# A two-layer block with a recurrent and a dilated-attention mixer: the first half of attention's output projection enters the planned order, and the conditioning loads are woven in further apart

## The chip, the cores and the metric

The kernel runs on one core of a Trainium2 chip. The metric is the device time of one execution in microseconds (us). Three runs of the kernel before gave 1509.72, 1512.40 and 1514.42 us; the median is 1512.4 us.

## What is computed

512 tokens of 1024 features pass through two layers. Layer 0 mixes with a gated linear recurrence (HGRN), layer 1 with an attention in which each of 8 heads has three groups (a near window and two strided ones) whose outputs are merged by their softmax sums. Each layer ends in a SwiGLU feed-forward net with 2816 hidden features. A vector `c` conditions both layers: `ada_w` turns it into six vectors of 1024 a layer (a shift, a scale and a gate for the mixer, and the same three for the feed-forward net).

```
cond = silu(c)
for layer in (0, 1):
    sh1, sc1, g1, sh2, sc2, g2 = split(cond @ ada_w[layer] + ada_b[layer], 6)
    u = rms_norm(h, norm_g[layer, 0]) * (1.0 + sc1) + sh1
    y = hgrn2_mixer(u, ...) if layer == 0 else dilated_attention_mixer(u, ...)
    h = h + (1.0 + g1) * rms_norm(y, norm_g[layer, 1])
    u = rms_norm(h, norm_g[layer, 2]) * (1.0 + sc2) + sh2
    y = (silu(gate) * up) @ ffn_w_out[layer]      # gate, up = split(u @ ffn_w_in[layer])
    h = h + (1.0 + g2) * rms_norm(y, norm_g[layer, 3])

def dilated_attention_mixer(u, cos, sin, w_in, w_out):
    proj = (u @ w_in).reshape(B, S, N_GROUPS, 3, ATT_HEADS, ATT_HEAD_DIM)
    for gi, (window, dilation) in enumerate(DILATED_GROUPS):
        q, k, v = rope(proj[:, :, gi, 0]) * scale, rope(proj[:, :, gi, 1]), proj[:, :, gi, 2]
        o_g, lse_g = dilated_group_attention(q, k, v, window, dilation)
    wts = softmax(stack(lses), axis=0)
    o = einsum('gbsh,gbshd->bshd', wts, stack(outs))
    return o.reshape(B, S, D_MODEL) @ w_out
```

## The kernel before

**Number format.** Every large product runs on TensorE (PE) in three passes of single-precision parts: a matrix `x` is cut into a high part (a cast, on ScalarE, ACT) and a low part (the difference, on VectorE, DVE), and `three` issues high·high, high·low and low·high into one PSUM bank. So each weight needs a load, a cast and a subtraction before PE can use it, and each operand of the output projection needs one cast (`oh`, a head's high part) and one subtraction (`ol`, its low part, named `oT` in the trace because it takes the place of an `oT` tile).

**Weights.** `items` is one list for the whole kernel: the order in which loads of about 1 MB are issued on SyncE's queue (SP) into a ring of two places called `raw`. A load starts only when the last reader of the item two places ahead in the list is done. Kinds of items are `w` (1 MB at once), `quarters`, `half`, `rows` and `ada`. An `ada` item is conditioning work: 1 MB of `ada_w`, four multiply-and-adds of 128x512 on DVE (lines 390 and 392; lines 1965 and 1967 within the plan). Behind every second `ada` comes a sum over the partitions on GpSimd (POOL), `partition_all_reduce` (line 394, or 1970 in the plan), and then four small turns into a column on DVE (line 404) or, for a gate, a `rows` load and two adds. `weave(ws, others, first, every)` strews the groups of `others` among the weights `ws`: one behind each `every`-th weight.

**Stages**, in the profile's time: the recurrence of layer 0 with its output turn (to about 300 us), its feed-forward net (to about 700 us), attention's products (q, k and v for 3 groups and 8 heads) and heads from about 740 to 1103 us, attention's output turn (1103 to about 1170 us), and the second feed-forward net.

**The recurrence's output turn.** `mixer_out` multiplies the eight heads (kt = 0 to 7) by the output weights; the last two heads still come through `core_c`/`core_d` while the first products run. `core_d` needs a mean square over a head raised to the power -1/2, which POOL does with `pow` (line 590, tile `orr`); a vector op on DVE (tile `aT`, line 1615) follows and PE turns the result (line 1622). A lone row `ISA` on POOL in the orders below is the instruction that changes POOL's loaded program between `partition_all_reduce` and `pow`.

**Attention's order.** An object `plan` is given every task of attention with its engine, an estimated cost and what it reads and writes, and derives one fixed order for each engine from it. Scores, merges, flips (turns on PE) and sums of a head are added at `ticks`, one for each q/k unit of groups 1 and 2. The plan ends with the last q/k products of head 7 and two of the four output weights. The rest, the "tail", is written by hand in `mixer_out` (its `else` branch and the dictionary `tail`): first half of the output turn, `y0` (four banks, one for each 128 tokens, first 512 columns), eight products kt for each; between them what is left of heads 6 and 7: the sums `pv_n(6)`, the scores `scores(7, 2)`, merges, flips and sums of head 7, and the way back of `h` from its place in memory (`back`). `y1` is the second half of the columns; its first bank is worked before kt = 7. The high parts `oh` stand in two places: three where the operand parts `up` were, and five that open when the q/k places (`mkx`) close behind kt = 0.

Of the kernel before, what the change touches and what calls it, by code (L numbers as in the profile page):

```python
# [10 lines left out]
F32 = mybir.dt.float32  # L11
F32R = mybir.dt.float32r
# [4 lines left out]
P = 128  # L17
# [274 lines left out]
def block_kernel(tc, x, c, positions, ada_w, ada_b, norm_g, hgrn_w_in, lower, hgrn_norm_g, hgrn_w_out,  # L292
# [8 lines left out]
    with ExitStack() as ctx:  # L301
# [250 lines left out]
        woven(late[:6], 2)  # L552
# [4 lines left out]
        woven(late[6:], 2)  # L557
        items += [wtok(attn_w_out[0], kq, hf * 512) for hf in range(2) for kq in range(2)]
# [126 lines left out]
        def mixer_out(oT, otp, groups, gate, l, side, close, tail=None):  # L685


            aux = ExitStack()
            oh, ol = [], []

            def parts(n):
                uid[0] += 1
                pp = aux.enter_context(tc.tile_pool(name=f"parts{uid[0]}", bufs=1, side=bass.opposite_side(side)))
                place = not oh
                for _ in range(n):
                    oh.append(fresh(pp, [P, S], f"oh{len(oh)}", 1, F32R))
                if place:
                    pp.tile([P, 72], F32, name=f"pad{uid[0]}")

            def cut(kt):  # L700
                ol.append(fresh(otp, [P, S], *(("oT", 7) if kt < 7 else ("oT_late", 2)), F32R))
                split(oh[kt], ol[kt], oT[kt])

            parts(groups[0])
            y0 = [bank("mm") for _ in range(NT)]
            y1 = {}
# [12 lines left out]
            if tail is None:  # L719
                for kt in range(KT):  # L720
                    if kt % 4 == 0:
                        w = st.take()
                    cut(kt)
# [3 lines left out]
            else:  # L727
                with tc.manual_schedule(engines=ORDERED):
                    for kt in range(3):
                        cut(kt)  # L730
                    for kt in range(KT):
                        if kt % 4 == 0:
                            w = st.take(0)
                        if kt == KT - 1:
                            ws = [st.take(0), st.take(0)]
                            mm(0, range(7))
                        for t in range(NT):
                            prods(y0[t], t, kt, w)
                        if kt == 0:
                            for fn in tail[-1]:  # L740
                                fn()
                            parts(groups[1])
                        if kt < 4:
                            cut(kt + 3)
                        for fn in tail.get(kt, ()):
                            fn()
                        if kt == 6:
                            cut(7)
                        if kt in (4, 5):
                            for hi_f, lo_f in st.pieces(2, True):  # L750
                                hi_f()
                                lo_f()
                            st.fill()
# [7 lines left out]
            mm(0, range(8) if tail is None else (7,))  # L761
# [912 lines left out]
        first = mixer_out(oT, otp, (8,), gates.pop((0, 2)), 0, "left", lambda: None)  # L1674
# [277 lines left out]
        acc_of = {}  # L1952
# [49 lines left out]
        def products(cost, dst, key, terms, begin, reads):  # L2002


            def go():
                todo = [p for t in terms() for p in t]
                for i, (x, y) in enumerate(todo):
                    pe.matmul(dst(), x, y, start=begin and i == 0, stop=i == len(todo) - 1, skip_group_check=True)  # L2008
            PE(cost, go, reads, [key])
# [399 lines left out]
        steps, after = [], []  # L2409
# [19 lines left out]
        for _ in range(2):  # L2429
            raw, p = next_weights(), plan.place("hl", 3, lambda: st.part_tiles(0))  # L2430
            for n in range(2):
                two = slice(n * 1024, n * 1024 + 1024)
                ACT(1.0, lambda raw=raw, p=p, two=two: act.copy(p.t[0][:, two], raw.t[:, two]), [raw()], [p("h", n)], goal=clock[0])
                DVE(1.15, lambda raw=raw, p=p, two=two: dve.tensor_sub(p.t[1][:, two], raw.t[:, two], p.t[0][:, two].bitcast(F32)),
                    [raw(), p("h", n)], [p("l", n)], goal=clock[0])
            done_with_raw()
            after.append(p)
        with tc.manual_schedule(engines=ORDERED | {mybir.EngineType.SP}):
            planned = plan.run()
        st.ready += [tuple(p.t) for p in after]  # L2440
        st.done, st.taken = at_item[0], st.taken + sum(k == "qk" and not by_seven(g) for k, g, _ in order)
        for st_ in heads.values():
            for name, p in st_.items():
                if isinstance(p, Place):
                    st_[name] = p.t
        for name, p in gates.items():
            if isinstance(p, Place):
                gates[name] = p.t
        upx.close()
# [36 lines left out]
```

## Time and profile before

| | before |
|---|---|
| median of 3 runs (lowest, highest) | 1512.4 us (1509.72, 1514.42) |
| the profiled execution: its time, its span | 1514.89 us, 1513.2 us |
| mean granted TensorE clock | 0.992 |
| PE busy | 1485.4 us, 98% |
| DVE, ACT, POOL busy | 1111.0, 795.5, 198.8 us |
| 20 us stretches in which PE is least busy | 280 to 300 us, 1100 to 1120 us, 800 to 820 us |

The span runs from the first to the last instruction; the execution's time has 1.7 us around it. PE is busy in 98% of the span, so the time can be read as PE's work plus the places where PE stands still, plus those where its granted clock is low; the list of PE's waits names each place with the engine and the line that ended it.

### The profile page before, as it was taken

Reading aid. Unit: us, or ns where it says so; the run is one execution under the profiler, and the core shown is the slowest. Engines: PE = TensorE matmul, PEld = TensorE weight load, DVE = VectorE, ACT = ScalarE, POOL = GpSimd, SP = SyncE. Lnnn points to the kernel's source line nnn. Section 1 sums busy time; section 2 is a strip of 40 time slices with the busy share of each in tenths; the row PEclk is TensorE's granted clock in tenths of the full one; section 3 lists DMA queues with packets and bytes.
Section 4 is the critical chain, followed back from the end, with each engine's and each line's share of the span. In section 5 each row is a group of like instructions: output and inputs, shape, how many; then the busy total and the mean of one; then the engine's idle time right before and its main releaser. Section 6 shows DMA issues by size and latency. Waiting matters only on the chain. (4 is left out here: it accounts for less than half of the span.)

```text
span 1513.2 us, 25135 instructions
## 1 busy us (share of the span) xinstructions
PE 1485.4 (98%) x9807; PEld 1329.2 (88%) x9807; DVE 1111.0 (73%) x1906; ACT 795.5 (53%) x1472; POOL 198.8 (13%) x174
## 2 busy tenths in 40 slices
PE   8999999899999999999999999999999999999998
PEld 6777888788999987888998999999978899999886
DVE  4587868387788876768798888888766978887533
ACT  4433443273555542366647777568865555555231
POOL 1011211130111101130001101001002211110100
PEclk9999999999999999999999999999999999999999
DMA  9554445215333347624244434443323333334531
GB/s 308 183 166 140 153 139 187 92 60 165 96 112 112 112 140 238 227 84 167 88 143 139 113 118 133 120 134 95 92 99 125 94 102 113 112 110 142 195 112 56
DMA packets 210152, 201.09 MB, mean 133 GB/s; under 512 B 8249, under 2 KB 167921, under 8 KB 209777
## 3 DMA queue, kind: packets, MB, share of 16 engines
q1 hardware_dynamic: 207056, 192.71, 40.9%
q10 hardware_dynamic: 1952, 6.65, 1.2%
q8 instruction: 77, 1.26, 0.4%
q0 software_dynamic: 1024, 0.13, 0.2%
q14 instruction: 43, 0.34, 0.1%
HBM read 192.31 MB, written 5.31 MB: 131 GB/s over the span
## 5 line engine op out<-in xcount | busy, mean ns | idle before, releaser
L89 ACT CAST hi<-raw 128x2048 fp32r<-128x2048 f32 x43 | 82.1, 1909 | 151.4 <-DMA raw<-in_ffn_w_out_dram 72.5
L90 DVE TENSOR_TENSOR lo<-raw,hi 128x2048 fp32r<-128x2048 f32 x43 | 101.8, 2371 | 62.5 <-ACT hi L89 62.3
L575 PE MATMUL ps_mm<-uh,hi 128*128 128x512 f32 (+1 forms) x400 | 146.4, 366 | 0.0
L576 PE MATMUL ps_mm<-ul,hi 128*128 128x512 f32 (+1 forms) x400 | 144.4, 361 | 1.0 <-DVE ul L675 1.0
L577 PE MATMUL ps_mm<-uh,lo 128*128 128x512 f32 (+1 forms) x400 | 144.7, 362 | 0.0
L2008 PE MATMUL ps_mm<-apart,hiq 128*128 128x256 f32 (+1 forms) x608 | 142.6, 327 | 0.0
L2008 PEld LDWEIGHTS ps_mm<-apart,hiq 128*128 128x128 f32 x608 | 99.9, 189 | 8.1
L2008 PE MATMUL ps_mm<-apart,loq 128*128 128x256 f32 (+1 forms) x304 | 98.0, 322 | 0.1
L990 PE MATMUL ps_mm<-th,loq 128*128 128x256 f32 x340 | 94.0, 277 | 0.0
L990 PE MATMUL ps_mm<-tl,hiq 128*128 128x256 f32 x340 | 94.0, 277 | 0.0
L990 PE MATMUL ps_mm<-th,hiq 128*128 128x256 f32 x340 | 94.0, 277 | 0.0
L981 DVE TENSOR_TENSOR loq<-raw,hiq 128x1024 fp32r<-128x1024 f32 x68 | 80.3, 1223 | 18.6 <-ACT hiq L977 18.6
L575 PEld LDWEIGHTS ps_mm<-uh,hi 128*128 128x128 f32 x400 | 75.6, 189 | 19.8 <-issue 8.4
L576 PEld LDWEIGHTS ps_mm<-ul,hi 128*128 128x128 f32 x400 | 75.6, 189 | 12.0 <-DVE ul L675 1.4
L577 PEld LDWEIGHTS ps_mm<-uh,lo 128*128 128x128 f32 x400 | 75.5, 189 | 11.4
L961 POOL TENSOR_TENSOR raw<-raw 128x512 f32<-128x512 f32 x34 | 44.9, 1320 | 305.3 <-DVE spare L957 149.6
L575 PE MATMUL ps_mm<-hi,oh 128*128 128x512 f32 x208 | 82.0, 394 | 1.0 <-ACT hi L89 1.0
L576 PE MATMUL ps_mm<-lo,oh 128*128 128x512 f32 x208 | 82.1, 395 | 0.2 <-DVE lo L90 0.2
L2008 PE MATMUL ps_mm<-uh,hiq 128*128 128x256 f32 x256 | 73.4, 287 | 3.7 <-ACT ps_mm L2100 2.5
L977 ACT CAST hiq<-raw 128x1024 fp32r<-128x1024 f32 x68 | 68.1, 1049 | 15.7 <-DVE raw L965 14.8
L2008 PE MATMUL ps_mm<-uh,loq 128*128 128x256 f32 x256 | 72.4, 283 | 0.2 <-DVE loq L2054 0.2
L2008 PE MATMUL ps_mm<-ul,hiq 128*128 128x256 f32 x256 | 72.4, 283 | 0.0
(513 smaller groups left out, 4668.1 us busy)
## 6 DMA issues: line engine op xcount, KB each, us to landing
raw<-in_ada_w_dram SPq DMA_DIRECT2D x40, 1024.0 KB, 5.2
raw<-in_ffn_w_in_dram SPq DMA_DIRECT2D x136, 256.0 KB, 3.6
raw<-in_ffn_w_out_dram SPq DMA_DIRECT2D x22, 1024.0 KB, 5.0
raw<-in_attn_w_in_dram SPq DMA_DIRECT2D x64, 256.0 KB, 4.8
raw<-in_hgrn_w_in_dram SPq DMA_DIRECT2D x12, 1024.0 KB, 5.3
raw<-in_attn_w_in_dram SPq DMA_DIRECT2D x12, 1024.0 KB, 5.2
raw<-in_ffn_w_in_dram SPq DMA_DIRECT2D x10, 1024.0 KB, 5.1
raw<-in_attn_w_in_dram SPq DMA_DIRECT2D x16, 512.0 KB, 5.3
```

The source lines that it names most:

```text
L89: self.nc.scalar.copy(hi, t)
L90: self.nc.vector.tensor_sub(lo, t, hi.bitcast(F32))
L575: pe.matmul(ps, ah, bh, start=start, stop=False, skip_group_check=part)
L576: pe.matmul(ps, ah, bl, start=False, stop=False, skip_group_check=part)
L577: pe.matmul(ps, al, bh, start=False, stop=stop, skip_group_check=part)
L961: pool.tensor_add(r[:, 2], r[:, 2], r[:, 0])
L977: act.copy(hi, src)
L981: dve.tensor_sub(lo, src, hi.bitcast(F32))
L990: pe.matmul(ps, w[x][:, a], us[kt][y], start=begin and kt + m == 0, stop=kt == 3 and m == 2, skip_group_check=True)
L2008: pe.matmul(dst(), x, y, start=begin and i == 0, stop=i == len(todo) - 1, skip_group_check=True)
```

## The change

Three lists are woven otherwise, and the tail becomes tasks of the plan.

1. In the recurrence's output turn the four loads of layer 1's FFN scale, `(1, 4)`, are called `shift`. The first of them now precedes the output weights, and the others follow one to each weight (before: two to a weight from the second on). The last column work goes into the plain weights of the feed-forward net, and that net's gate loads come one item later.
2. In attention four groups instead of six are woven into heads 1 to 4, one for each 2.5 items instead of 2; two into heads 5 to 7, one for each 3; the last two `ada` loads are woven into the four output weights.
3. The first half of attention's output turn is added to the plan: casts of the four output weights, the parts `oh`/`ol`, the products of `y0` and seven of `y1[0]`, the ways back of `h`. All eight high parts are in one place, that of `up` (`apart`), opened when all products of q, k and v (`of_units`) are done. What the plan holds of heads 6 and 7 comes at ticks inside this loop. `merged`, `flipped` and `sums` are the functions that the other heads already use, so head 7's merges run as scalings on ACT (before in the tail: on DVE), and its flips are copied on ACT.

```
-        items += weave(hg, ada_seq((0, 2), (0, 4), (0, 3)), 1)
-        items += weave(hg_o, [g for g in ada_seq((1, 4)) if g], 0, 0.5)
+        shift = ada_seq((1, 4))
+        items += weave(hg, ada_seq((0, 2), (0, 4), (0, 3)), 1) + shift[0]
+        items += weave(hg_o, shift[1:4], 0)
...
-        items += weave(f0a[:n0], gate_loads[:2] + [gate_fins[:1]], 2) + f0a[n0:]
+        items += weave(f0a[:n0], shift[5:] + gate_loads[:2] + [gate_fins[:1]], 2) + f0a[n0:]
...
-        woven(late[:6], 2)
+        woven(late[:4], 2.5)
...
-        woven(late[6:], 2)
-        items += [wtok(attn_w_out[0], kq, hf * 512) for hf in range(2) for kq in range(2)]
+        woven(late[4:6], 3)
+        out_w = [wtok(attn_w_out[0], kq, hf * 512) for hf in range(2) for kq in range(2)]
+        items += weave(out_w, late[6:], 0)
...
+        def out_weights():
             raw, p = next_weights(), plan.place("hl", 3, lambda: st.part_tiles(0))
             for n in range(2):
                 two = slice(n * 1024, n * 1024 + 1024)
+                ACT(1.0, lambda two=two: act.copy(p.t[0][:, two], raw.t[:, two]), [raw()], [p("h", n)])
+                DVE(1.15, lambda two=two: dve.tensor_sub(p.t[1][:, two], raw.t[:, two], p.t[0][:, two].bitcast(F32)), [raw(), p("h", n)], [p("l", n)])
             done_with_raw()
+            ws.append(p)
...
+        def out_cut(kt):
+            ACT(0.58, lambda: act.copy(oh[kt], oT[kt]), [("oT", kt), rows_of[kt]], [("oh", kt)])
...
+        out_weights()
+        out_weights()
+        open_parts(8, of_units, upx.close)
+        for kt in range(3):
+            out_cut(kt)
+        y0 = [mm_of() for _ in range(NT)]
+        last = ticks.n
+        for kt in range(KT):
+            if kt == 7:
+                y1[0] = mm_of("a")
+                for k in range(7):
+                    out_prods(y1[0], 0, k, ws[2 + k // 4])
+            for t in range(NT):
+                out_prods(y0[t], t, kt, ws[kt // 4])
+            for _ in range({0: 3, 2: 1, 4: 1, 5: 1, 6: 1}.get(kt, 0)):
+                ticks.tick()
+            if kt == 0:
+                come_back(0, [("PN", 0, t) for t in range(NT)])
+            if kt < 4:
+                out_cut(kt + 3)
...
+            if kt in (4, 5):
+                out_weights()
```

How the order moves, at three places. **POOL in the recurrence's output turn** (`shared` is the sum of one half of the conditioning vector, `orr` is the `pow` of heads 6 and 7). Before:

```order
L394 ISA
L394 ISA shared<-shared 128x512
L590 ISA
L590 TENSOR_TENSOR orr_2308<-rv_2309,expo 128x4
L394 ISA
L394 ISA shared<-shared 128x512
L590 ISA
L590 TENSOR_TENSOR orr_2342<-rv_2343,expo 128x4
```

With the change:

```order
L394 ISA
L394 ISA shared<-shared 128x512 x2
L592 ISA
L592 TENSOR_TENSOR orr_2315<-rv_2316,expo 128x4
L592 TENSOR_TENSOR orr_2349<-rv_2350,expo 128x4
```

Both sums now stand ahead of both `pow`, and one pair of program changes is gone; head 6's `pow` waits for the second sum.

**DVE at the start of attention's output turn** (`loq` is the low part of an output weight, `oT<-oT,oh` the low part of a head, `mR` the maxima of head 7's scores, `rot` and `shared` the rotary rows of head 7). Before:

```order
L2281 TENSOR_SCALAR nN_10183<-sN_10528 128x4
L2434 TENSOR_TENSOR loq_10843<-raw_10695,hiq_10842 128x1024
L2434 TENSOR_TENSOR loq_10931<-raw_10962,hiq_10930 128x1024
L572 TENSOR_TENSOR oT_11081<-oT_6093,oh_11071 128x512
L572 TENSOR_TENSOR oT_11084<-oT_6094,oh_11072 128x512
L572 TENSOR_TENSOR oT_11087<-oT_6095,oh_11073 128x512
L2434 TENSOR_TENSOR loq_10931<-raw_10962,hiq_10930 128x1024
```

With the change:

```order
L2256 TENSOR_SCALAR nN_10137<-sN_10530 128x4
L1939 TENSOR_SCALAR shared<-raw_10947,cond 128x512
L1941 SCALAR_TENSOR_TENSOR shared<-raw_10947,cond,shared 128x512 x2
L2426 TENSOR_TENSOR oT_11046<-oT_6093,oh_11018 128x512
L1941 SCALAR_TENSOR_TENSOR shared<-raw_10947,cond,shared 128x512
L1995 STREAM_SHUFFLE rot_10973<-shared 128x256
L1996 TENSOR_TENSOR rot_10973<-rot_10973,shared 128x256
L1997 TENSOR_TENSOR shared<-shared 128x256
L1998 TENSOR_TENSOR shared<-shared,rot_10973 128x256
L2412 TENSOR_TENSOR loq_10824<-raw_10682,hiq_10823 128x1024
L2426 TENSOR_TENSOR oT_11078<-oT_6094,oh_11019 128x512
```

Four steps of conditioning now stand around the first low part, and the second half of the first weight's low part and the rotation of head 7's rows stand ahead of the second. The second output weight (`raw_10962`, now `raw_11080`) comes some 25 instructions later.

**DVE in the middle of that turn**, where head 7's first merge (`wM`, `wE`, `wZ`) stands, with the change:

```order
L2412 TENSOR_TENSOR loq_10915<-raw_11080,hiq_10914 128x1024
L1941 SCALAR_TENSOR_TENSOR shared<-raw_11082,cond,shared 128x512
L2298 TENSOR_TENSOR wM_10835<-sR_10407,oR_10405 128x4
L2299 TENSOR_TENSOR wE_10895<-sR_10407,wM_10835 128x4
L2300 TENSOR_TENSOR wE_10895<-oR_10405,wM_10835 128x4
L1941 SCALAR_TENSOR_TENSOR shared<-raw_11082,cond,shared 128x512
L2412 TENSOR_TENSOR loq_10915<-raw_11080,hiq_10914 128x1024
```

Before, no conditioning stood here: the merge followed three low parts of heads.

```order
L572 TENSOR_TENSOR oT_11140<-oT_6096,oh_11135 128x512
L572 TENSOR_TENSOR oT_11155<-oT_6097,oh_11136 128x512
L572 TENSOR_TENSOR oT_11170<-oT_6098,oh_11137 128x512
L1834 TENSOR_TENSOR wM_11173<-sR_10429,oR_11120 128x4
L1835 TENSOR_TENSOR wE_11174<-sR_10429,wM_11173 128x4
L1836 TENSOR_TENSOR wE_11174<-oR_11120,wM_11173 128x4
```

The merge now stands behind the arrival of a second conditioning load (`raw_11082`), which the ring of two places lets start only behind an output weight.

More of the change, by code (lines that the diff above doesn't have):

```diff
@@ L760, in mixer_out @@
             n.gated(0, 0)
-            mm(0, range(8) if tail is None else (7,))
+            mm(0, range(8) if made is None else (7,))
             n.sq_y(0, 1)
@@ L2438, in block_kernel @@
+        while st.items[at_item[0]][0] in ("ada", "do", "rows"):
+            condition(st.items[at_item[0]])
+            at_item[0] += 1
         with tc.manual_schedule(engines=ORDERED | {mybir.EngineType.SP}):
             planned = plan.run()
[L2440 to L2445, printed above, removed]
```

113 lines of the change are left out of this document (51 added, 62 removed).

## The prediction

> **What bounds the kernel now.** First the page's table of busy time:
>
> ```profile
> PE 1485.4 (98%) x9807; PEld 1329.2 (88%) x9807; DVE 1111.0 (73%) x1906; ACT 795.5 (53%) x1472; POOL 198.8 (13%) x174
> ```
>
> PE stands still for 1513.2 - 1485.4 = 27.8 us of the span. The change removes no product, so it can only gain from those 27.8 us and from stretches at a low granted clock, and can only lose by making more of either. The list of PE's waits says where they are (engine, line, what ended the wait; us in all, times, longest):
>
> ```profile
> PE ps_a L1622 <- DVE aT L1615: 4.8, 1, 4.8
> PE ps_mm L2008 <- ACT ps_mm L2100: 2.5, 1, 2.5
> ...
> PE ps_mm L575 <- ACT qk L2112: 2.0, 1, 2.0
> ...
> PE ps_mm L2008 <- ACT ps_mm L2096: 1.1, 1, 1.1
> ...
> PE ps_mm L575 <- ACT oh L571: 0.9, 1, 0.9
> PE ps_mm L2008 <- DVE loq L2188: 0.8, 1, 0.8
> PE ps_a L2298 <- ACT h L2363: 0.7, 1, 0.7
> ```
>
> These seven lie in the three places that the change touches: the recurrence's output turn (4.8), attention's products (2.5, 1.1, 0.8) and the start of attention's output turn (2.0, 0.9, 0.7). I sum the change place by place. A difference of 0.3%, 4.5 us, is about what a measurement of this kernel can tell from no change.
>
> **Attention's output turn.** PE there, then the turn by stretches (length, busy time of PE, PEld, DVE, ACT, POOL, granted clock, DMA share, GB/s):
>
> ```profile
> 1103.09 0.93 PE L2355 MATMUL ps_a<-ident,h 128*128 128x128 f32 x7
> 1104.91 0.50 PE L575 MATMUL ps_mm<-hiq,oh 128*128 128x512 f32 x1 [0.89 <-ACT oh L571]
> 1106.32 1.91 PE L2298 MATMUL ps_a<-qk,qk 128*128 128x128 f32 x8 [0.68 <-ACT h L2363]
> 1111.92 0.50 PE L575 MATMUL ps_mm<-hiq,oh 128*128 128x512 f32 x1 [1.98 <-ACT qk L2112]
> ...
> 1146.91 0.39 PE L577 MATMUL ps_a<-hi,oT_late 128*128 128x512 f32 x1
> 1147.14 0.39 PE L575 MATMUL ps_a<-hi,oh 128*128 128x512 f32 x1
> ```
>
> ```profile
> 1106.00:1108.00 2.00, 1.68 (x9) 1.68 (x9) 1.79 (x4) 1.98 (x5) 0.00 (x0) 0.63 0.93 309
> 1108.00:1110.00 2.00, 1.94 (x6) 1.03 (x4) 1.97 (x8) 1.96 (x7) 0.00 (x0) 0.51 0.52 203
> ...
> 1112.00:1114.00 2.00, 2.00 (x9) 1.72 (x10) 0.00 (x0) 1.95 (x6) 0.00 (x0) 0.84 0.87 322
> 1114.00:1116.00 2.00, 2.00 (x12) 2.00 (x10) 0.00 (x0) 0.15 (x1) 0.00 (x0) 0.50 0.00 0
> 1116.00:1118.00 2.00, 2.00 (x14) 1.91 (x14) 1.00 (x4) 0.00 (x0) 0.55 (x1) 0.81 0.02 1
> ```
>
> From the last flips of the planned part (1103.09) to the first product of the second token group's second half (1147.14) pass 44.05 us. Three waits take 0.89 + 0.68 + 1.98 = 3.55 us. The low clock costs, in each stretch PE's busy time by what the clock lacks of 1, 0.62 + 0.95 + 0.32 + 1.00 + 0.38 = 3.27 us. Without both, the same instructions take 37.2 us, so -6.8 us is the most that this place can give.
>
> What the planned order puts in their place: the 1.98 us wait was for a bank that still held a q/k product, which ACT read behind four exponentials; with the change ACT's reads of those banks stand around the first `oh`, ahead of the exponentials, so this wait goes. The first products of kt = 0 now stand behind the scores and `pv_n(6)`, which gives `oh` and `ol` the time of those. The costs that come in are DVE's and POOL's:
>
> ```profile
> 1116.74 0.69 DVE L1901 TENSOR_TENSOR oT_late<-oT_late,ps_b 128x512 f32<-128x512 f32 x1 [5.16 <-PE ps_b L1900]
> ```
>
> ```profile
> 795.73 2.32 DVE L1967 SCALAR_TENSOR_TENSOR shared<-raw,cond,shared 128x512 f32<-128x512 f32 x3
> ```
>
> ```profile
> raw<-in_ada_w_dram SPq DMA_DIRECT2D x40, 1024.0 KB, 5.2
> ```
>
> Each of the two conditioning loads adds four steps of 0.77 us on DVE (the row above, 2.32 / 3), so 6.2 us, and some 2 us of column work. DVE has idle time for it here, 5.16 us in the first row alone. What counts is the queue. Walking each engine's new order with the durations of before: `pv_n(6)` waits about 0.5 us for the copy of its flips, since ACT casts the first `oh` ahead of it; the second `ol`, behind four steps of conditioning, the rotation of head 7's rows and the second half of the first weight, comes about 0.4 us after PE asks. Head 7's first merge stands behind the second conditioning load. That load waits on SP behind an output weight, which waits for the place of the first (free at about 1110); two loads of 1 MB from there, 5.2 us the first and about 3.3 us more the second, land it at about 1118.5; the merge and its scalings end at about 1124.6, just when PE comes to head 7's flips. The last two weights then land some 4 us ahead of their products. The sum over the partitions that follows at about 1124.4 meets the low part of head 6, the third cost. What it does to DVE shows earlier (POOL's sum, then DVE's rows beside and behind it):
>
> ```profile
> 867.57 3.23 POOL L1970 PARTITION_ALL_REDUCE shared<-shared  x1 [12.75 <-DVE shared L1967]
> ```
>
> ```profile
> 867.86 2.22 DVE L2021 TENSOR_TENSOR rot<-rot,shared 128x256 f32<-128x256 f32 x1
> 870.01 0.41 DVE L2022 TENSOR_TENSOR shared<-shared 128x256 f32<-128x256 f32 x1
> ```
>
> An instruction of 0.41 us takes 2.22 us beside the sum, and ends 0.7 us before it. So head 6's low part is late by about 2 us, and PE, which has 1 us of other work there, waits about 1.1 us. Together 0.5 + 0.4 + 1.1 = 2.0 us: the place costs -6.8 + 2.0 = **-4.8 us**. Its bounds are -6.8 (nothing waits) and +2.9, from the row below: DVE's 23.9 us of work between 1103 and 1141 become 23.9 + 8.2 + 2.1 (beside the sum) - 2.2 (head 7's scalings, now on ACT) = 32.0 us. Its idle time is 38 - 23.9 = 14.1 us now; if only the 5.16 us of it go, the 38 us become 32.0 + 8.9 = 40.9.
>
> ```profile
> 1103.00:1141.00 38.00, 34.45 (x178) 29.22 (x177) 23.85 (x66) 22.23 (x49) 2.63 (x4) 0.91 0.38 128
> ```
>
> [...]
>
> **The recurrence's output turn.** POOL and PE before:
>
> ```profile
> 268.26 1.68 POOL L590 TENSOR_TENSOR orr<-rv,expo 128x4 f32<-128x4 f32 x1 [9.17 <-DVE rv L589]
> 275.87 3.25 POOL L394 PARTITION_ALL_REDUCE shared<-shared  x1 [5.94 <-PE ps_b L1608]
> 286.30 1.05 POOL L590 TENSOR_TENSOR orr<-rv,expo 128x4 f32<-128x4 f32 x1 [7.18 <-issue]
> ```
>
> ```profile
> 273.44 0.61 PE L1606 MATMUL ps_b<-v_tok,aT 128*128 128x128 f32 x4
> ...
> 288.13 1.12 PE L1622 MATMUL ps_a<-ident,aT 128*128 128x128 f32 x4 [4.79 <-DVE aT L1615]
> ```
>
> Between the end of the sum (279.12) and the `pow` lie 7.18 us in which POOL waits for nothing else: the price of the program change. Before, head 6 had its `pow` ahead of the second sum and only head 7 paid. Now the order is sum, sum, change, `pow`, `pow`, and head 6 pays. The second sum needs the fourth conditioning load. By the same kind of walk its place in the ring comes free at about 258.8; with 5.2 us of landing and DVE's queue behind it, a weight's low part of 2.3 us among it, its last step ends at about 271.3. The sum then takes 3.25, the change 7.18, the `pow` 1.05 to 1.68, DVE's product 0.69 (as the 128x512 one in the row at 1116.74): 283.5 to 284.1. PE comes to the turn at about 277.4 (273.44, 1.5 us of `core_c`, eleven products at 0.23 us, as 1146.91 to 1147.14), and waits 6.1 to 6.7 us; I take 6.7 instead of 4.79, since the `pow` right behind a change was the longer one. Head 7 then finds its value ready, and the clock behind the wait I take as before. Cost **+2 us**; bounds -1 (the load lands early and DVE's queue is clear) and +4 (landing 2 us later).
>
> **Attention's products.** The 2.52 us wait:
>
> ```profile
> 805.59 0.39 PE L2008 MATMUL ps_mm<-uh,hiq 128*128 128x256 f32 x1 [2.52 <-ACT ps_mm L2100]
> ```
>
> ```profile
> 800.67 1.84 DVE L2021 TENSOR_TENSOR rot<-rot,shared 128x256 f32<-128x256 f32 x1
> ```
>
> ```profile
> 807.00:809.00 2.00, 2.00 (x12) 2.00 (x11) 1.93 (x4) 1.53 (x6) 0.00 (x0) 0.50 0.54 142
> ```
>
> ACT's copy of a bank stood behind copies of rotary rows that DVE finished late: its first step took 1.84 us instead of 0.4 beside POOL's sum. The wait and the low clock in the last row (2.00 us at 0.50) cost 3.5 us; with the waits of 1.1 and 0.8 the block can give 5.4. With six loads instead of eight, DVE has 6.2 us less here, the sums fall elsewhere, and the weights behind the second load start one item earlier. But sums and loads remain, and one may hit another narrow place. I take the 3.5 as gained and 1.0 as returned (the size of the second wait): **-2.5 us**; bounds -5.4 and +2.5 (one more wait like the first).
>
> [...]
>
> Where the gate loads of the first feed-forward net come one item later, PE works with no wait in the list, and the weights come at about the same time: 0.
>
> **Sum.** -4.8 + 2 - 2.5 = -5.3 us: the profiled execution's 1514.89 us would be 1509.6, and the median 1512.4 us **1507**.
>
> **The rivals.**
> - *The small terms all fall well*: the recurrence's wait does not grow (0), the tail loses 0.5, the block's waits go (-5): 1501. For it: each cost worked out above is a wait of about 1 us, within the error of the walk. Against it: three would have to vanish.
> - *The tail is given back in part*: the second conditioning load lands 2 to 3 us later, as it would behind two full landings of 5.2 us (1120.4), and head 7's flips wait with it; -2.5 there, +2 and -0.5 elsewhere: 1511.4. For it: the merge has no slack. Against it: two loads in flight landed faster than one by one.
> - *DVE becomes the bound of the tail*, and the kernel is slower. Its place: the queue that now mixes eight steps of conditioning, four weights' halves, eight low parts and head 7's merges. Its price: the +2.9 above, with the clock halved once behind its waits (1.7, as from 1112 to 1118), +2 in the recurrence and 0 in the block: 1512.4 + 2.9 + 1.7 + 2 = 1519. It decides if DVE keeps about 9 of its 14.1 us of idle time, because each instruction waits for a load or for PE in an order made from estimates. For it: the estimates know neither the clock nor the 2 us beside a sum. Against it: most of the new work is there early and could fill that idle time.
>
> **How the numbers follow.** Forecast 0.40, all well 0.20, given back in part 0.18, DVE-bound 0.22. Faster by over 4.5 us means under 1507.9: 0.28 of the forecast's 0.40, all 0.20 and 0.02 make 0.50. Slower means over 1516.9: 0.20 of the DVE case and 0.05 of given back make 0.25; the rest is 0.25. The range of 8 in 10 goes from 1500 to 1518; the forecast's own is 1503 to 1511.
>
> **What would show it.** Right: in the list of PE's waits the one for ACT `qk` is gone, the turn lasts about 39 us between the same two products, the clock there stays at 1; on POOL two sums follow each other and PE's wait for `aT` is about 7 us; around 805 us PE does not stand. Wrong: PE waits of over 1 us for `loq` or `oT` low parts or for head 7's flips in the turn, with DVE waiting for `raw`; or a wait of over 2 us at a new place between 780 and 1000 us.

## The result, and the profile after

The changed kernel takes 1511.49 us (median of 12 runs, 1508.44 to 1513.67) against 1513.76 us for the kernel before (12 runs, 1509.72 to 1516.32): a ratio of 0.9987 with a 95% interval of 0.9976 to 0.9998. That is 2.3 us less. The interval lies just below 1, and the gain is smaller than the 0.3% (4.5 us) which the prediction took as the least that can be told from no change. The forecast was 5.3 us less.

The profiled execution took 1511.48 us, its span 1509.5 us at a mean granted clock of 0.995 (before 1514.89, 1513.2 and 0.992). The page's table of busy time after the change:

```profile
PE 1481.1 (98%) x9807; PEld 1324.4 (88%) x9807; DVE 1108.2 (73%) x1896; ACT 799.6 (53%) x1482; POOL 200.7 (13%) x174
```

PE now stands still for 1509.5 - 1481.1 = 28.4 us, and before for 27.8: the change took no idle time away from PE on balance. Its busy time fell by 4.3 us for the same 9807 products, because less of it ran at a low clock (mean granted clock 0.995 instead of 0.992). The list of PE's waits (engine, line, what ended the wait; us in all, times, longest; line numbers here are some 26 lower than before):

```profile
PE ps_a L1596 <- DVE aT L1589: 5.1, 1, 5.1
PE ps_mm L1982 <- ACT ps_mm L2071: 2.9, 2, 2.1
...
PE ps_a L2330 <- DVE sN L2253: 1.8, 1, 1.8
...
PE ps_a L2330 <- ACT h L2319: 0.9, 1, 0.9
```

Of the seven waits quoted before, two at the start of attention's output turn are gone: the 2.0 us for ACT's `qk` and the 0.9 us for `oh`. The third one there, 0.7 us for `h`, is down to 0.2. The wait for `aT` in the recurrence is 5.1 us instead of 4.8. Attention's products have a wait of 2.1 us of the same kind as the one of 2.5 before, and a new one of 1.8 us.

To see where the time went I cut the span at five of PE's products, the same ones in each kernel. In the kernel before (PE's timeline; start, duration, then the idle time ahead of it and what ended it):

```profile
25.57 0.74 PE L1345 MATMUL ps_a<-hi,uh 128*128 128x512 f32 x2 [0.61 <-ACT uh L1320]
330.54 1.10 PE L656 MATMUL ps_b<-ident,xn 128*128 128x128 f32 x8 [0.56 <-DVE xn L650]
599.19 0.50 PE L575 MATMUL ps_mm<-hi,oh 128*128 128x512 f32 x1 [0.99 <-ACT hi L89]
```

and with the change:

```profile
27.49 0.74 PE L1319 MATMUL ps_a<-hi,uh 128*128 128x512 f32 x2 [0.61 <-ACT uh L1294]
331.69 1.09 PE L658 MATMUL ps_b<-ident,xn 128*128 128x128 f32 x8 [0.56 <-DVE xn L652]
600.55 0.50 PE L577 MATMUL ps_mm<-hi,oh 128*128 128x512 f32 x1 [0.72 <-ACT hi L89]
1104.49 0.93 PE L2330 MATMUL ps_a<-ident,h 128*128 128x128 f32 x7
1143.25 0.39 PE L579 MATMUL ps_a<-hiq,oT_late 128*128 128x512 f32 x1
```

The last two marks of the kernel before are the products at 1103.09 and 1146.91 that the prediction quotes. The same marks in the other kernels give this table (us; "attention" is the stage from the third mark to the last flips, attention's products and heads with the end of the first feed-forward net; "turn" is the first half of attention's output turn). Labels are those of the experiments below.

| kernel | start | recurrence | first FFN | attention | turn | rest |
|---|---|---|---|---|---|---|
| before | 25.57 | 304.97 | 268.65 | 503.90 | 43.82 | 366.3 |
| before, second profile (e2) | 25.29 | 305.59 | 268.72 | 503.35 | 42.26 | 366.3 |
| the change | 27.49 | 304.20 | 268.86 | 503.94 | 38.76 | 366.3 |
| the change, second (e1) | 26.63 | 305.38 | 269.22 | 503.93 | 38.29 | 366.4 |
| the change, third (e11) | 26.25 | 305.59 | 268.71 | 506.64 | 39.07 | 366.3 |
| e3: planned turn, lists of before | 25.57 | 305.51 | 268.76 | 501.24 | 37.60 | 366.0 |
| e4: recurrence's list alone | 25.74 | 304.63 | 269.20 | 500.99 | 43.81 | 366.0 |
| e6: e3 and conditioning in the turn | 25.31 | 305.55 | 268.41 | 500.61 | 38.86 | 366.2 |
| e7: the change without four sums | 25.38 | 304.72 | 268.04 | 499.01 | 37.23 | 366.3 |
| e12: e3 without four sums | 25.45 | 305.35 | 268.35 | 499.33 | 37.73 | 366.0 |

From the mean of the two profiles before to the mean of the three after: turn -4.3, recurrence -0.2, first FFN +0.2, attention +1.2, start +1.4, rest 0. They add to -1.7 us, as the spans do (1512.35 to 1510.63).

**The turn after.** PE's rows there, then two stretches (length; busy time of PE, PEld, DVE, ACT, POOL; granted clock; DMA share; GB/s):

```profile
1105.62 1.16 PE L2273 MATMUL ps_a<-qk,qk 128*128 128x128 f32 x8 [0.20 <-ACT h L2338]
1107.02 0.71 PE L2364 MATMUL ps_b<-h,V 128*128 128x128 f32 x4 [0.24 <-ACT h L2338]
...
1132.26 0.66 PE L2330 MATMUL ps_a<-ident,h 128*128 128x128 f32 x4 [0.91 <-ACT h L2319]
```

```profile
1104.00:1112.00 8.00, 7.56 (x50) 6.55 (x49) 7.23 (x14) 7.37 (x18) 0.00 (x0) 1.00 0.34 118
1112.00:1120.00 8.00, 8.00 (x41) 6.77 (x40) 6.56 (x25) 8.00 (x23) 1.86 (x3) 1.00 0.46 149
```

The low clock (0.50 to 0.84 in most stretches between 1106 and 1118 before) is gone. Of the three old waits two are gone, and the one of head 7's scores is 0.20 us instead of 0.68. What came in is 0.24 us ahead of `pv_n(6)` and 0.91 us at head 7's flips. The last one has its cause on DVE and POOL:

```profile
1126.69 2.20 DVE L2302 TENSOR_TENSOR wZ<-wE,sN 128x4 f32<-128x4 f32 x1
1128.82 0.15 DVE L2303 TENSOR_TENSOR wZ<-wE,oN 128x4 f32<-128x4 f32 x1
```

```profile
1126.27 3.60 POOL L1944 PARTITION_ALL_REDUCE shared<-shared  x1 [4.13 <-DVE shared L1941]
```

An addition of 128x4, 0.15 us long in the next row, took 2.20 us beside the sum over the partitions. Head 7's second merge was late by that, ACT's scaling and PE's flips behind it.

### The profile page after: what moved, and what is told of

Its sections match the earlier page's. It is cut to its first block, busy times and chain, and to the rows that moved or that the text cites. A ratio compares the mean times of both kernels' runs of the same rounds, so it can differ in the third digit from the quotient of the medians.

```text
span 1509.5 us, 25145 instructions
## 1 busy us (share of the span) xinstructions
PE 1481.1 (98%) x9807; PEld 1324.4 (88%) x9807; DVE 1108.2 (73%) x1896; ACT 799.6 (53%) x1482; POOL 200.7 (13%) x174
```

## The experiments

All ratios are against the kernel before, with a 95% interval; each kernel's number of runs stands behind its median. Short diffs are against the kernel named.

### e1, e2, e11: the change and the kernel before, profiled again

No edit. For the second profile of the change:

> The changed kernel once more, unchanged, for a second profile and more runs. The first pair of profiles differs by -3.7 us of span: +1.9 at the start (PE reaches the first products of the recurrence at 27.49 us instead of 25.57, with the same instructions in the same order), -0.8 in the recurrence's output turn, about 0 in the attention block, -5.1 in attention's output turn. Theory A: the start is chance, the rest is the change. Then this profile starts those products anywhere between 25 and 28 us, the turn again takes 39.0 us between its two marks (44.05 before), and the ratio comes out near 0.9963 (-5.6 us). Theory B: the start belongs to the changed kernel, or the stages vary from run to run by as much as they gained. Then the start is again near 27.5 us, or the turn's length differs by over 1 us from 39.0, and the ratio stays near 0.9985 (-2.3 us).

It took 1511.39 us (12 runs), ratio 0.9982 (0.9971 to 0.9994). For the second profile of the kernel before:

> The kernel before once more, for a second profile of it. Theory A: the turn takes 44 us again, PE waits 4.8 us for aT and 2.5 us at about 805 us, and the start lies anywhere between 25 and 28 us. Theory B (start belongs to the kernel): the start lies at 25.6 us again within 0.3. Theory B (stages vary): the turn lies over 1 us off 44.05, or the wait of 2.5 us is gone or elsewhere.

It took 1513.17 us (one run). Here is the place of the 2.52 us wait on PE, and DVE's step ahead of it:

```profile
804.39 0.39 PE L2008 MATMUL ps_mm<-uh,hiq 128*128 128x256 f32 x1 [0.91 <-ACT ps_mm L2100]
```

```profile
799.46 1.84 DVE L2021 TENSOR_TENSOR rot<-rot,shared 128x256 f32<-128x256 f32 x1
```

DVE's step is stretched to 1.84 us just as in the first profile, but it began 1.2 us earlier (799.46 against 800.67), and PE waited 0.91 us, not 2.52. The wait that I priced at 3.5 us with its low clock was one draw of a near miss. This profile has a draw of its own elsewhere: PE waited 1.83 us at 976.59 (0.76 in the first profile), and the clock from 976 to 980 was 0.61. A third profile of the change:

> A third profile of the changed kernel, for the start alone: the five kernels with the changed conditioning lists in attention reached their first products at 27.5, 26.6, 27.9 and 25.4 us, the six others at 25.3 to 25.7. If the start belongs to the lists, 26.5 to 28 us again; if it is chance, 25.3 to 25.7 is as likely.

It took 1514.43 us (one run); its attention stage is 2.7 us longer than in the other two. The same stretch behind the wait at 897 (here 898) in the first profile of the change and in this one, in this order:

```profile
901.00:905.00 4.00, 4.00 (x38) 4.00 (x37) 3.39 (x12) 3.87 (x10) 0.00 (x0) 1.00 0.57 162
```

```profile
901.00:905.00 4.00, 4.00 (x27) 4.00 (x26) 3.50 (x9) 3.25 (x8) 0.00 (x0) 0.68 0.38 110
```

With a wait of 1.83 us ahead of it in both, PE did 38 products in 4 us at full clock once, and 27 at 0.68 the other time. So one and the same program differs by 2 to 3 us in this stage alone.

### e3: only the planned turn

The change with the three lists of the kernel before:

```diff
-        shift = ada_seq((1, 4))
-        items += weave(hg, ada_seq((0, 2), (0, 4), (0, 3)), 1) + shift[0]
-        items += weave(hg_o, shift[1:4], 0)
+        items += weave(hg, ada_seq((0, 2), (0, 4), (0, 3)), 1)
+        items += weave(hg_o, [g for g in ada_seq((1, 4)) if g], 0, 0.5)
...
-        woven(late[:4], 2.5)
+        woven(late[:6], 2)
...
-        woven(late[4:6], 3)
+        woven(late[6:], 2)
...
-        items += weave(out_w, late[6:], 0)
+        items += out_w
```

(The first FFN's gate loads go back too.)

> Attention's output turn is planned as in the change, and the three lists of conditioning are as before, so no conditioning load stands in the turn. Theory A (the turn's gain is its own): -5 to -6.8 us, ratio 0.9955 to 0.9967, the turn at 37.5 to 39 us, since DVE has 8 us less there than in the change. Theory B (the turn gains only because conditioning elsewhere is spread): the turn stays above 41 us or the attention block ahead of it gets waits of over 2 us more, ratio 0.998 or above.

It took 1507.17 us (6 runs), ratio 0.9956 (0.9939 to 0.9973): faster than the whole change by 4.3 us. The turn is 37.6 us. The prediction's floor of 37.2 us ends at a product 0.23 us behind the table's mark, so by the table it is 37.0, and e3 comes within 0.6 us of it, with one wait of 0.2 us left. So the planned turn does what was forecast, and the lists of the change give part of it back.

### e4: only the recurrence's list

The kernel before with the change's two lines on `shift` and its line on the first FFN.

> Only the recurrence's list is changed (two sums in a row on POOL ahead of both pow), all else as before. By the prediction's step: +2 us, ratio 1.0013, PE's wait for aT 6.7 us. By the profile of the change: wait 5.1 us and a shorter stretch at low clock, -0.8 us, ratio 0.9995. If the start belongs to the changed lists, this kernel starts its first products at 27.5 us as well.

It took 1513.52 us (12 runs), ratio 1.0001 (0.9989 to 1.0013). PE's wait for `aT` is 5.2 us and the stage 304.63 us: this part of the change is worth nothing either way. This kernel's attention stage took 501.0 us though nothing of it was edited: it has neither the low clock of the first profile (at 807) nor that of e2 (at 977). That again shows how far the stage moves by itself.

### e5 and e6: where attention's conditioning stands

e5 is the change with the last four conditioning groups in heads 5 to 7, none in the turn:

```diff
-        woven(late[4:6], 3)
+        woven(late[4:], 2)
...
-        items += weave(out_w, late[6:], 0)
+        items += out_w
```

> The change, but with the last two conditioning loads back among heads 5 to 7 (groups 5 and on, one for each 2 items), so that none stands in attention's output turn; the wider spacing in heads 1 to 4 and the recurrence's list stay. Theory C: the wider spacing puts sums on POOL beside two-input work of DVE that PE waits for, at about 807 and 893 us. Then the waits of 2.1 and 1.8 us there stay, the turn falls from 38.5 to 37.6 us, ratio 0.997 to 0.998. Theory D: what is lost against e3 (0.9956) is lost to the conditioning in the turn. Then this kernel comes to 0.9955 to 0.9965.

It took 1516.1 us (8 runs), ratio 1.0022 (1.0012 to 1.0032). The turn took 38.2 us, but a wait of 3.60 us came up in heads 5 to 7, with the clock at 0.61 behind it:

```profile
1026.93 0.79 PE L1982 MATMUL ps_mm<-apart,hiq 128*128 128x256 f32 x2 [3.60 <-ACT xs L2096]
```

```profile
1025.68 0.17 DVE L2298 TENSOR_TENSOR wM<-sN,oN 128x4 f32<-128x4 f32 x1 [6.28 <-DMA oN<-scr]
```

DVE stood for 6.28 us until a transfer of a head's sums came back; the sums of POOL nearest to it stand at 893.67 and 1036.20. The waits at 815 and 897 us stayed (2.42 and 1.71 us), as the theory of the sums had it, but the new wait hides what the conditioning in the turn is worth. e6 asks that without it. It keeps before's spacing in heads 1 to 4 and has conditioning in the turn, none in heads 5 to 7 (diff against e3):

```diff
-        woven(late[6:], 2)
+        woven([], 1)
...
-        items += out_w
+        items += weave(out_w, late[6:], 0)
```

> The planned turn with the lists of before for the recurrence and heads 1 to 4 (six groups, one for each 2 items), none in heads 5 to 7 and the last two loads among the output weights as in the change. Theory C: the block's waits are as before (0.9 at 804, 1.2, 1.2 to 1.8 us), the turn lasts 38.5 us, ratio 0.9962 to 0.997. Theory D: the turn or the stage behind it gives back 3 us and more, ratio 0.998 or above.

It took 1506.95 us (5 runs), ratio 0.9964 (0.9951 to 0.9976). Against e3 the conditioning in the turn costs 38.86 - 37.60 = 1.3 us. The turn of e3 and of e6 by one window each, in this order:

```profile
1101.00:1139.00 38.00, 37.66 (x206) 31.77 (x205) 20.93 (x57) 26.79 (x59) 2.64 (x4) 1.00 0.49 167
```

```profile
1101.00:1139.00 38.00, 36.80 (x196) 30.97 (x197) 28.44 (x73) 26.23 (x57) 6.22 (x5) 1.00 0.63 208
```

DVE has 7.5 us more to do and POOL a sum, yet PE is busy for only 0.9 us less of this window, at full clock: DVE has the room. So of the change's three lists it is the one for heads 1 to 7 that costs: between e6 and the change stand 4.2 us in the attention stage (500.61 against the mean of 504.84).

### e7 and e12: without POOL's sums

Two kernels test whether POOL's sums are the cause. Both leave out the four sums over the partitions in attention's plan, e7 from the change and e12 from e3, so that layer 1's mixer gate and FFN shift stay unsummed.

```diff
-                    POOL(3.3, lambda: pool.partition_all_reduce(a.t, a.t, P, bass.bass_isa.ReduceOp.add), w=[a()])
+                    POOL(3.3, lambda: None, w=[a()])
```

> The change, without the four sums over the partitions on POOL within attention's plan: layer 1's mixer gate and FFN shift are left unsummed, so the output is not the reference's; the order of everything else is the same. Theory C: the waits at 815 us (2.1) and 897 us (1.8) go, and DVE's L2033 there takes 0.7 us instead of 2.6 and 3.3; the attention block gains 3 to 5 us and the turn up to 1; ratio 0.9945 to 0.996. Rival (the waits come from the order alone, DVE's load or a late weight): waits stay within 0.5 us of what they were, ratio 0.998.

> e3 (planned turn, lists of before) without the four sums on POOL within attention's plan; layer 1's mixer gate and FFN shift are left unsummed, so the output is not the reference's. Theory C (the wider spacing costs only through where the sums fall): with no sums the lists no longer matter, so the attention block (from the wait at 600 us to the last flips of the planned products) comes to e7's 499 us, ratio 0.993 to 0.995, where e3 has 501.2 and the change 503.9. Rival (the wider spacing costs by itself, by loads or DVE steps at worse places): then e12's block is 2 us and more shorter than e7's 499.

e7 took 1503.11 us (5 runs), ratio 0.9936 (0.9924 to 0.9948); e12 took 1504.41 us (6 runs), ratio 0.9952 (0.9934 to 0.9969). Without sums the two lists are equal: 499.0 and 499.3 us in attention, 37.2 and 37.7 in the turn. With them the change's list takes 504.8 us (mean of three) and e3 501.2. So the sums cost the change 5.8 us in this stage and e3 about 2, and without sums the change's spacing costs nothing. e7, e12 and e3 have one profile each, and the stage moves by 2 to 3 us from one profile to the next; but the medians say the same. With the sums the change's list costs 4.3 us (the change against e3), and without them nothing (1503.1 against 1504.4).

What the sums do in the change, step by step. POOL:

```profile
807.55 3.58 POOL L1944 PARTITION_ALL_REDUCE shared<-shared  x1 [49.29 <-DVE shared L1941]
...
892.96 3.18 POOL L1944 PARTITION_ALL_REDUCE shared<-shared  x1
...
1037.53 3.42 POOL L1944 PARTITION_ALL_REDUCE shared<-shared  x1
```

DVE:

```profile
808.04 2.62 DVE L2033 TENSOR_TENSOR raw<-raw 128x512 f32<-128x512 f32 x1
...
812.07 0.69 DVE L2033 TENSOR_TENSOR raw<-raw 128x512 f32<-128x512 f32 x1
...
892.43 3.27 DVE L2033 TENSOR_TENSOR raw<-raw 128x512 f32<-128x512 f32 x1
...
1037.78 2.73 DVE L2029 TENSOR_TENSOR loq<-raw,hiq 128x512 fp32r<-128x512 f32 x1
```

ACT and then PE:

```profile
810.69 0.62 ACT L2028 CAST hiq<-raw 128x512 fp32r<-128x512 f32 x1 [2.70 <-DVE raw L2033]
...
814.73 0.36 ACT L2071 COPY ps_mm<-ps_mm 128x256 f32<-128x256 f32 x1
...
896.54 1.71 ACT L2314 ACTIVATE h<-h,wE 128x256 f32<-128x256 f32 x4 [3.02 <-DVE wE L2306]
```

```profile
815.15 0.38 PE L1982 MATMUL ps_mm<-uh,hiq 128*128 128x256 f32 x1 [2.14 <-ACT ps_mm L2071]
...
897.20 1.43 PE L2330 MATMUL ps_a<-ident,h 128*128 128x128 f32 x4 [1.83 <-DVE sN L2253]
...
1044.14 0.38 PE L1982 MATMUL ps_mm<-uh,hiq 128*128 128x256 f32 x1 [0.74 <-ACT ps_mm L2071]
```

The step on line 2033 takes 0.69 us (row at 812.07). Beside the sum at 807.55 it takes 2.62; ACT's cast waits 2.70 us for it, its copy of a bank comes late, and PE waits 2.14. Beside the sum at 892.96 it takes 3.27; head merges stand behind it on DVE, ACT's scalings wait 3.02, and PE's flips 1.83. The third sum holds a step on line 2029 for 2.73 us (0.69 at 1034.58), ACT's copy of a bank ends only at 1044.09, and PE waits 0.74. In e7 line 2033 has no long step (shortest, median and longest ns of all 64):

```profile
L2033 DVE TENSOR_TENSOR raw<-raw x64: 683/692/695, 712.7 to 1084.4; 128x512 f32<-128x512 f32 x64
```

and no wait of PE for ACT's copy on line 2071 or for the flips is over 0.3 us. All three profiles of the change have all three waits: 2.14, 1.83 and 0.74; 2.01, 1.71 and 1.11; 2.43, 1.83 and 1.19. They add to 4.7, 4.8 and 5.5 us, most of the 5.8. A sum lengthens DVE's step with before's spacing as well (in the kernel before to 1.84 us at 800.67, 2.22 at 867.86 and 2.11 at 1021.97), but at places where PE waits less (0.8 to 1.1 us behind the first of them in e2, e3, e4 and e6).

### e8, e9, e10: the wait in the recurrence's output turn

PE's wait for `aT` was said to be POOL's sum and program change ahead of `pow`. If so, it goes when no sum stands there. e8 moves the four loads of `(1, 4)` into the second half of the first FFN (against e3):

```diff
-        items += weave(hg_o, [g for g in ada_seq((1, 4)) if g], 0, 0.5)
+        items += hg_o
...
-        rest = ada_seq((1, 1), (1, 0))
-        items += weave(f0b, gate + [gate_fins[1:] + rest[0]] + rest[1:], 0, 0.8)
+        rest = ada_seq((1, 4), (1, 1), (1, 0))
+        items += weave(f0b, gate + [gate_fins[1:] + rest[0]] + rest[1:], 0, 0.6)
```

> e3 with all four loads of layer 1's FFN scale moved out of the recurrence's output turn into the second half of the first feed-forward net (conditioning groups there one for each 0.6 weights instead of 0.8). POOL then does both pow with no sum and no program change between. Theory: PE's wait for aT (4.8 to 5.9 us in all profiles) and the low clock behind it (2 to 3 us) go: ratio 0.9956 - 0.005 = 0.9906 (-14 us). Rival: the feed-forward net's second half, with three conditioning loads to two weights, waits for weights or DVE by 3 us or more: ratio 0.993 or above.

It took 1515.18 us (12 runs), ratio 1.0017 (1.0004 to 1.0029). The mechanism is confirmed. e8 also takes the loads' steps off DVE, but DVE was not what PE waited for: in e3 it stood idle for 5.94 us itself until `orr` came. In e8 POOL's two `pow` stand without a change between,

```profile
266.64 1.01 POOL L591 TENSOR_TENSOR orr<-rv,expo 128x4 f32<-128x4 f32 x1 [31.22 <-DVE rv L590]
275.33 1.01 POOL L591 TENSOR_TENSOR orr<-rv,expo 128x4 f32<-128x4 f32 x1 [7.68 <-DVE rv L590]
```

and PE does not wait for `aT`. The recurrence takes 297.2 us, 8.3 less than in e3. But the loads come where weights are already late: from the second mark to the last flips this kernel takes 17.2 us more than e3 (787.2 against 770.0), with waits such as these between 330 and 720 us:

```profile
PE ps_mm L576 <- ACT hi L89: 5.6, 2, 3.7
PE ps_mm L577 <- DVE lo L90: 3.1, 3, 2.0
```

e9 puts the loads among the quarters of that net's first half instead (against e3, with `hg_o` plain as in e8):

```diff
-        items += weave(f0a[:n0], gate_loads[:2] + [gate_fins[:1]], 2) + f0a[n0:]
+        items += weave(f0a[:n0], gate_loads[:2] + [gate_fins[:1]], 2) + weave(f0a[n0:], ada_seq((1, 4)), 1, 2.5)
```

> As e8 (the planned turn, before's lists in attention, no sum between or ahead of the recurrence's two pow), but the four loads of layer 1's FFN scale go among the up and gate weights of the first feed-forward net, one for each 2.5 of them, where PE stood nowhere between 340 and 580 us and DVE is 73 to 82% busy. Theory: the 8.3 us that e8 gained by 323 us stay (e8 lost 16 us behind 571 us, where its loads stood three to two weights): e3's 0.9956 - 0.0055 = 0.990, PE's wait for aT under 0.5 us. Rival: DVE or the sums make PE wait in the feed-forward net as in e8: 0.993 or above.

It took 1535.95 us (4 runs), ratio 1.0141 (1.0128 to 1.0154). This stage keeps its own work in the memory that holds the sums' accumulators, so the two wait for each other (four waits of 14.9 us in all, two of 8.8), and by the code layer 1's scale vector is overwritten in part. It says nothing on the question beyond that this place is taken.

e10 leaves the loads where they are and lets PE multiply and sum that vector, as it does for three vectors of layer 0 (against e3):

```diff
-        by_pe = lambda l, v: l == 0 and v in (2, 3, 4)
+        by_pe = lambda l, v: (l, v) in ((0, 2), (0, 3), (0, 4), (1, 4))
```

> e3 with the four loads of layer 1's FFN scale left in the recurrence's output turn, but multiplied and summed on PE (as the kernel does for three vectors of layer 0) instead of on DVE and POOL. No sum and no program change on POOL either. Theory: the wait for aT goes (-8 us), PE pays about 4 us for 16 products of 128x512: ratio 0.9956 - 0.0026 = 0.993. Rival: the wait comes from the loads or from DVE and not from POOL's program; then it stays at 4 us or more and the ratio is 0.997 or above.

It took 1514.6 us (12 runs), ratio 1.0012 (1.0 to 1.0023). The wait for `aT` falls to 2.18 us. No sum and no change stands ahead of the second `pow` there (at 270.33, right behind its value), but PE has run out of other work at 270.0 us, in e3 at 283.3. PE now also waits for the loads itself:

```profile
272.21 0.63 PE L1595 MATMUL ps_a<-ident,aT 128*128 128x128 f32 x4 [2.18 <-DVE aT L1588]
275.18 1.93 PE L370 MATMUL ps_mm<-raw,cond_tiles 128*32 128x512 f32 x8 [2.34 <-DMA raw<-in_ada_w_dram]
```

The granted clock is 0.64 between 272 and 280 us, and the recurrence takes 7.7 us more than in e3.

## Why the prediction was wrong, point by point

The time, 1511.5 us, lies inside the range of 1500 to 1518 and just past the upper end of the forecast's own (1511). The forecast of a clear gain, -5.3 us, failed: it is -2.3 by the medians. The case that came true is nearest to "given back in part" (1511.4) in its time and in none of its places, so that nearness is luck.

- **Attention's output turn: right, in size and largely in place.** Forecast -4.8 us, between its own two marks 44.05 to 38.98 = -5.1 in the first pair of profiles, -4.3 between the means of the stage table. e3 comes within 0.6 us of the floor. The floor took all three old waits as gone; 0.20 us of the scores' 0.68 stayed. Of the three new waits, `pv_n(6)` cost 0.24 us where I took 0.5; the second `ol` none where I took 0.4; and the sum of POOL 0.6 to 0.9 where I took 1.1, through head 7's second merge and not through the low part of head 6.
- **"Given back in part" by a late second load: fell.** The load did not hold the merge. Two loads in flight took 9.3 us here and not two full landings of 5.2: the output weight, issued at 1107.79, landed in 6.6 us, and the conditioning load, issued at 1110.71, in 6.4, at 1117.1. DVE's row at 1120.10, `wM`, had waited for head 7's sums and not for `raw`:

```profile
1120.10 0.17 DVE L2298 TENSOR_TENSOR wM<-sR,oR 128x4 f32<-128x4 f32 x1 [0.96 <-DMA oR<-scr]
```

- **DVE as the bound of the turn: fell.** The place came out 4.3 us below the kernel before, not the 2.9 + 1.7 above it of that rival; the conditioning in it costs 1.3 us (e3 against e6). The 1.7 stood for a clock halved once behind the waits; in the change's profile the granted clock was 1.00 from 1104 to 1142 us.
- **The recurrence's output turn: mechanism right, the term mis-sized.** POOL's order came as said, two sums, the change, two `pow`:

```profile
271.73 3.23 POOL L394 PARTITION_ALL_REDUCE shared<-shared  x1 [18.09 <-DVE rv L591]
282.73 1.05 POOL L592 TENSOR_TENSOR orr<-rv,expo 128x4 f32<-128x4 f32 x1 [7.77 <-issue]
285.33 1.01 POOL L592 TENSOR_TENSOR orr<-rv,expo 128x4 f32<-128x4 f32 x1 [1.55 <-DVE rv L591]
```

  I took a wait of 6.7 us instead of 4.79. It was 5.1, 6.0 and 6.0 in the three profiles of the change and 5.2 in e4, against 4.8 to 5.6 with the list of before (before, e2, e3, e6, e12), and the stage did not grow (305.1 against 305.3 us): +2 was -0.2. Four sizes were off. The `pow` took 1.05 us, not the 1.68 I used, which was a misreading: of the two `pow` before, the one that the change held up (286.30) was the short one. The change (in the first profile `MODIFY_POOL_CONFIG` in POOL's queue at 274.9, at the end of the second sum, and idle time from there to the `pow`) took 7.8 to 8.4 us in the three profiles, not 7.2. The sum began at 271.73 in a run whose start was 1.9 us later, so 1.5 us earlier than my walk had it. And the low clock that I took as before cost less: PE's busy time from 280 to 290 times what the clock lacks of 1 is 1.9 us (2.1 and 2.3 in e1 and e11), against 2.6 before.
- **Attention's products: the step that failed.** The prediction took "the 3.5 as gained and 1.0 as returned": -2.5 us. It came to +1.2 against the two profiles before, +2.5 against the mean of the four kernels' profiles with before's spacing (before, e2, e3, e4: 502.4). Two errors lie in it. First, the 3.5 us were there in one profile of five with before's spacing: in e2, e3, e4 and e6 PE's wait at that place is 0.8 to 1.1 us without a low clock. Second, I named the risk (sums and loads may "hit another narrow place") and priced it at 1.0 in all; all three sums left in heads 1 to 7 hit such places, with waits of 2.14, 1.83 and 0.74 us in the first profile and much the same in the other two. e7 and e12 show the cause: without sums both lists take the same time.
- **The first FFN's gate loads: right**, +0.2 forecast as 0.
- **The start: not foreseen.** PE's first mark came at 26.25 to 27.49 us in the change's three profiles, 27.90 in e5 and 27.39 in e9, and 25.3 to 25.7 in all other profiles. The instructions up to there are the same and stand in the same order; e7, with all of the change's lists, has 25.38, and e9, late, has the lists of before in attention. So it is not a rule of the lists. What differs is the granted clock behind the first products. Before, and then with the change:

```profile
16.00:20.00 4.00, 3.99 (x21) 2.91 (x20) 3.90 (x6) 2.71 (x6) 1.06 (x1) 0.79 1.13 328
20.00:24.00 4.00, 4.00 (x32) 2.68 (x31) 2.37 (x3) 1.09 (x2) 0.73 (x1) 1.00 1.13 326
```

```profile
16.00:20.00 4.00, 3.62 (x12) 2.83 (x13) 3.82 (x6) 2.18 (x5) 0.83 (x1) 0.50 1.13 328
20.00:24.00 4.00, 4.00 (x17) 2.80 (x20) 2.15 (x3) 0.81 (x1) 0.73 (x1) 0.71 1.13 326
```

  By the same reckoning the low clock takes 0.8 us before and 3.0 here, and the start came 1.9 us later. All five late profiles have 0.50 to 0.57 from 16 to 20 us, all others 0.72 to 1.00. Why it falls there in these runs stays open, and with it 1.4 us of the sum.

## What to carry to other kernels

A wait read from one profile is a draw (2.52 us in one profile of the kernel before, 0.91 at the same place in the next): before a near miss is counted as a gain, profile the kernel again, and price only what comes back. When short work that holds up another engine is moved, ask for each new place what the instruction beside it feeds; here the cost of the sums lay not in their number but in which DVE step each one met. When a change has several parts, run each alone: the part that carried the gain, the planned turn, is worth about 6 us by itself (e3, 1507.2 us), and the lists that came with it cost most of that.

## What the runs showed of the hardware that I had not expected

- A sum over the partitions of 128x512 on POOL (3.2 to 3.6 us) held one DVE instruction in each of the places shown, a small one too: 128x512 from 0.69 to 2.62, 2.73 and 3.27 us, 128x4 from 0.15 to 2.20. It need not have two inputs: before, a `TENSOR_SCALAR` of 128x4 (`nN`, 0.16 us elsewhere) took 2.11 us at 1021.97, beside the sum at 1021.82. DVE's step at 808.04 ended 0.47 us ahead of the recorded end of the sum at 807.55 (810.66 against 811.13), and the one at 892.43 was held though it began 0.53 us ahead of its sum. What in POOL's sum holds DVE, and from when to when, these runs do not show.
- Whether the granted clock fell behind a wait of some 2 us was a toss. It fell after 2.52 us (before, at 805: 0.64 from 805 to 809), 2.42 us (e5, at 815: 0.57 from 815 to 819) and 1.83 us (e2, at 977: 0.61 from 976 to 980). It did not after 2.14, 2.01 and 2.43 us (the change's three profiles at 815: 1.00 from 815 to 819) and 1.76 us (e12, at 974: products of 128x256 every 0.12 us after it as before it). After the wait at 897 (1.83, 1.71 and 1.83 us in the change's profiles) it was 1.00, 1.00 and 0.68 from 901 to 905.
- The sum and the program change ahead of a `pow` cost the recurrence about 8 us: in e3 PE's wait of 5.42 us and the low clock behind it (0.78 from 285 to 290 us and 0.54 from 290 to 295, 2.6 us by PE's busy time) make 8.0, and without them the stage is 8.3 us shorter (e8). The wait is the longest in PE's list, and both ways tried to be rid of it (e8, e10) made the kernel slower than e3, by 8.0 and 7.4 us.
